# Average pooling 2x2x2: eight loads through one ring, five of them issued by GpSimd

## The chip, the cores and the metric

The kernel runs on one core of a Trainium2 chip. The metric is device time in microseconds, the median of repeated executions. One execution of each kernel is also recorded by the hardware profiler. Its span goes from the first recorded instruction to the last; DMA transfers that are still landing after the last instruction are outside the span but inside the device time.

## The reference

The input `x` has shape (8, 32, 32, 32, 32) in float32, 33.55 MB. Each output element is the mean of a 2x2x2 window; windows don't overlap, so the output is (8, 32, 16, 16, 16), 4.19 MB.

```python
for i in range(out_d):
    for j in range(out_h):
        for k in range(out_w):
            window = x[:, :, 2*i:2*i + 2, 2*j:2*j + 2, 2*k:2*k + 2]
            result[:, :, i, j, k] = np.mean(window, axis=(-3, -2, -1))
```

## The kernel before

Batch and channel together give 256 rows of 128 KB. They are taken as two halves, `t = 0` and `t = 1`, of 128 rows, one row per partition. Along a row the data is cut into units; a unit of `kb` KB is `kb` KB in each of the 128 partitions (`KF` is 1 KB in float32 elements). In the diff and below, (t, k0, kb) is a unit: its half, where it starts in the row, and its length, both in KB.

The list `plan` has eight entries of 32 KB. Each takes one of five buffers of 32 KB from the pool `pin` (`tin` in the profile), 160 KB per partition in all. The last two entries are loaded as two pieces of 16 KB each. So there are ten loads, six of 4 MB and four of 2 MB, all issued by the SP engine on one queue in the order of `plan`. The sixth load and those after it wait until VectorE has finished with the buffer that they overwrite.

For each loaded piece, `pool_unit` runs three steps on VectorE, in place: L58 adds the two planes of a pair (depth), L62 adds neighbours (width), and L65 adds the two rows of a pair (height), scales by 0.125, and writes to the output buffer `obuf0` or `obuf1`. L65 shows in the profile as two entries, the operation itself and a short read of an accumulator that goes to `dummy`. Each of the three steps counts VectorE's semaphore up by one. The scheduler of the framework may move steps of one unit ahead of another's.

Three stores follow on SP, behind all loads: 12 KB of half 1, 16 KB of half 0, and the last 4 KB of half 1. In the output, 1 KB stands for 8 KB of the input, so that 12 KB of half 1 need its first 96 KB of input.

After the program is compiled, its instruction lists are edited by hand: the first load is moved ahead of the opening barrier of the engines, so that SP issues it at once; and the final waits for the three stores are moved behind the closing barrier.

Of the kernel before, what the change touches and what calls it, by code (L numbers as in the profile page):

```python
# [1 line left out]

# [4 lines left out]

F32 = mybir.dt.float32
KF = 256


@with_exitstack
def pool_rows(
    ctx: ExitStack,
    tc: tile.TileContext,
    x: bass.AP,
    kernel_size: int,
    out: bass.AP,
):
    nc = tc.nc  # L20
    assert kernel_size == 2, "only kernel_size == 2 supported"

    B, C, D, H, W = x.shape
    P = nc.NUM_PARTITIONS
    assert (B * C, D, H, W) == (2 * P, 32, 32, 32)
    add = mybir.AluOpType.add

    xv = x.rearrange("b c d h w -> (b c) (d h w)")  # L30
    ov = out.rearrange("b c d h w -> (b c) (d h w)")

    pool_in = ctx.enter_context(tc.tile_pool(name="pin", bufs=5))
    pool_out = ctx.enter_context(tc.tile_pool(name="pout", bufs=1))
    obuf = [pool_out.tile([P, 16 * KF], F32, name=f"obuf{t}") for t in range(2)]
    dummy = pool_out.tile([P, 1], F32, name="dummy")


    plan = [
        (0, 0, (32,)),
        (0, 32, (32,)),
        (0, 64, (32,)),
        (0, 96, (32,)),
        (1, 0, (32,)),
        (1, 32, (32,)),
        (1, 64, (16, 16)),
        (1, 96, (16, 16)),  # L50
    ]

    def pool_unit(buf, t, k0, kb):

        od = kb // 8
        a = buf.rearrange("p (o dd e) -> p o dd e", o=od, dd=2)
        b = buf[:, :od * 1024]
        nc.vector.tensor_add(  # L58
            out=b.rearrange("p (o e) -> p o e", o=od), in0=a[:, :, 0], in1=a[:, :, 1])
        bv = b.rearrange("p (e ww) -> p e ww", ww=2)  # L60
        c = buf[:, od * 1024:od * 1536]
        nc.vector.tensor_add(out=c, in0=bv[:, :, 0], in1=bv[:, :, 1])  # L62
        cv = c.rearrange("p (j hh k) -> p j hh k", hh=2, k=16)
        o0 = k0 * KF // 8
        nc.vector.tensor_tensor_reduce(  # L65
            out=obuf[t][:, o0:o0 + od * 256].rearrange("p (j k) -> p j k", k=16),
            in0=cv[:, :, 0], in1=cv[:, :, 1],
            scale=0.125, scalar=0.0, op0=add, op1=add, accum_out=dummy[:, :],
        )

    for t, k0, parts in plan:
        tin = pool_in.tile([P, 32 * KF], F32, tag="tin", name="tin")
        views = []
        o = 0
        for kb in parts:
            v = tin[:, o * KF:(o + kb) * KF]
            nc.sync.dma_start(
                out=v, in_=xv[t * P:(t + 1) * P, (k0 + o) * KF:(k0 + o + kb) * KF])
            views.append((v, k0 + o, kb))
            o += kb  # L80
        for v, k, kb in views:
            pool_unit(v, t, k, kb)

    for t, k0, kb in [(1, 0, 12), (0, 0, 16), (1, 12, 4)]:
        nc.sync.dma_start(
            out=ov[t * P:(t + 1) * P, k0 * KF:(k0 + kb) * KF],
            in_=obuf[t][:, k0 * KF:(k0 + kb) * KF],
        )  # L90


def kernel(tc: tile.TileContext, x: bass.AP, kernel_size: int, out: bass.AP):
    nc = tc.nc
    pool_rows(tc, x, kernel_size, out)
    tc.close()
    tc.compile()  # L97
    blocks = nc.main_func.blocks

    opening, program = blocks[0].instructions, blocks[tc.starting_block_idx].instructions
    load = next(i for i in program if isinstance(i, mybir.InstDMACopy))
    assert load.engine == nc.sync.engine
    barrier = next(
        n for n, i in enumerate(opening)
        if i.engine == load.engine and isinstance(i, mybir.InstDrain))
    program.remove(load)
    opening.insert(barrier, load)

    closing = blocks[-1].instructions
    stores = [
        i for i in program
        if isinstance(i, mybir.InstDMACopy) and "out_" in i.outs[0].memref]
    kept = [u.id for i in stores for u in i.sync_info.on_update]
    final = next(
        i for i in closing  # L120
        if i.engine == nc.sync.engine and isinstance(i, mybir.InstDrain))
    waits = {w.id: w for w in final.sync_info.on_wait}
    closing[closing.index(final)] = mybir.InstDrain(
        name=final.name, engine=final.engine, ins=[], outs=[], is_reset_sema=False,
        sync_info=mybir.SyncInfo(
            on_wait=[w for n, w in waits.items() if n not in kept], on_update=[]))


    reset = next(
        n for n, i in enumerate(closing)  # L130
        if isinstance(i, mybir.InstDrain) and i.is_reset_sema)
    first, stop = closing[reset].reset_range_start, closing[reset].reset_range_stop
    assert isinstance(closing[reset + 1], mybir.InstISA)
    while len(closing) > reset:
        closing.pop()
    n = first
    while n < stop:
        m = n
        while m < stop and m not in kept:
            m += 1  # L140
        if m > n:
            closing.append(mybir.InstDrain(
                name=nc.get_next_instruction_name(), engine=nc.gpsimd.engine, ins=[], outs=[],
                is_reset_sema=True, reset_range_start=n, reset_range_stop=m))
            nc.gpsimd.sem_clear(range(n, m))
        n = m + 1
    for n in kept:
        w = waits[n]
        closing.append(mybir.InstEventSemaphore(
            name=nc.get_next_instruction_name(), engine=nc.sync.engine, ins=[], outs=[],  # L150
            sync_info=mybir.SyncInfo(
                on_wait=[w],
                on_update=[mybir.SyncUpdate(
                    sync_type="semaphore", id=n, ant_name=w.ant_name,
                    update_mode="sem-sub-imm", update_value=w.wait_value)])))


# [1 line left out]
_INS = ['x', 'kernel_size']  # L159
_OUTS = [((8, 32, 16, 16, 16), 'float32')]  # L160

_NUMBERS = {'kernel_size': 2}


# [26 lines left out]
```

## Time and profile before

| what | value |
|---|---|
| device time, median of 15 runs | 91.41 us (91.29 to 91.92) |
| device time of the profiled execution | 91.3 us |
| its span | 86.4 us |
| VectorE busy | 64.0 us |
| GpSimd busy | 0.2 us (four memsets at the start) |
| first load landed, first VectorE step | 12.08 us |
| median issue to landing, 4 MB loads / 2 MB loads | 34.9 / 38.0 us |
| last VectorE step ends | about 85.2 us |

How to read it: the last instruction in the span is on VectorE; the stores that depend on it are issued by SP and land after the span. The time from issue to landing of a load is mostly time in the queue behind earlier loads, since SP issues several ahead.

### The profile page before, as it was taken

Reading aid. Unit: us, or ns where it says so; the run is one execution under the profiler, and the core shown is the slowest. Engines: PE = TensorE matmul, PEld = TensorE weight load, DVE = VectorE, ACT = ScalarE, POOL = GpSimd, SP = SyncE. Lnnn points to the kernel's source line nnn. Section 1 sums busy time; section 2 is a strip of 40 time slices with the busy share of each in tenths; the row PEclk is TensorE's granted clock in tenths of the full one; section 3 lists DMA queues with packets and bytes.
Section 4 is the critical chain, followed back from the end, with each engine's and each line's share of the span. In section 5 each row is a group of like instructions: output and inputs, shape, how many; then the busy total and the mean of one; then the engine's idle time right before and its main releaser. Section 6 shows DMA issues by size and latency. Waiting matters only on the chain.

```text
span 86.4 us, 89 instructions
## 1 busy us (share of the span) xinstructions
DVE 64.0 (74%) x40; POOL 0.2 (0%) x4
## 2 busy tenths in 40 slices
DVE  0000049993999749992999749992999999999994
POOL 0000000000000000000000000000000000000000
DMA  8979997999979998899979999798999999999999
GB/s 243 410 334 470 486 486 319 410 486 486 455 303 455 486 486 379 364 470 486 486 303 425 486 486 455 303 455 379 470 394 455 410 440 432 417 432 398 444 440 463
DMA packets 1679, 36.68 MB, mean 425 GB/s; under 512 B 176, under 2 KB 176, under 8 KB 176
## 3 DMA queue, kind: packets, MB, share of 16 engines
q1 hardware_dynamic: 1679, 36.68, 99.5%
HBM read 33.55 MB, written 4.19 MB: 437 GB/s over the span
## 4 chain that ended last, share of the span: by engine, by line
DMA 61%; DVE 37%; issue 0%; DVEq 0%
DMA tin<-in_x_dram 61%; DVE tin L58 21%; DVE tin L62 11%; DVE obuf L65 6%; DVE dummy L65 0%; DVEq L97 0%
## 5 line engine op out<-in xcount | busy, mean ns | idle before, releaser
L58 DVE TENSOR_TENSOR tin<-tin 128x4096 f32<-128x4096 f32 (+1 forms) x10 | 35.7, 3569 | 20.6 <-DMA tin<-in_x_dram 20.6
L62 DVE TENSOR_TENSOR tin<-tin 128x2048 f32<-128x2048 f32 (+1 forms) x10 | 18.6, 1864 | 0.3
L65 DVE CUSTOM_DVE_ANT_1 obuf<-tin 128x1024 f32<-128x1024 f32 (+1 forms) x10 | 10.1, 1010 | 0.3
L65 DVE DVE_READ_ACCUMULATOR2_ANT dummy<- 128x1 f32 x10 | 0.8, 82 | 0.0
L172 POOL MEMSET const-uint8-127<- 128x1 uint8 x1 | 0.1, 102 | 0.0
L172 POOL MEMSET const-bfloat16-1.0<- 128x1 bf16 x1 | 0.1, 101 | 0.0
L172 POOL MEMSET const-float32-0.0<- 128x1 f32 x1 | 0.1, 98 | 0.2 <-issue 0.2
L172 POOL MEMSET const-float32-1.0<- 128x1 f32 x1 | 0.1, 98 | 0.0
## 6 DMA issues: line engine op xcount, KB each, us to landing
tin<-in_x_dram SPq DMA_DIRECT2D x6, 4096.0 KB, 34.9
tin<-in_x_dram SPq DMA_DIRECT2D x4, 2048.0 KB, 38.0
out_dram<-obuf SPq DMA_DIRECT2D x1, 2048.0 KB, 11.5
out_dram<-obuf SPq DMA_DIRECT2D x1, 1536.0 KB, 7.0
out_dram<-obuf SPq DMA_DIRECT2D x1, 512.0 KB, 4.7
```

Of the source, the lines that this page charges most:

```text
L58: nc.vector.tensor_add(out=b.rearrange("p (o e) -> p o e", o=od), in0=a[:, :, 0], in1=a[:, :, 1])
L62: nc.vector.tensor_add(out=c, in0=bv[:, :, 0], in1=bv[:, :, 1])
L65: nc.vector.tensor_tensor_reduce(out=obuf[t][:, o0:o0 + od * 256].rearrange("p (j k) -> p j k", k=16), in0=cv[:, :, 0], in1=cv[:, :, 1], s ...
L172: nc = _bacc.Bacc("TRN2", target_bir_lowering=False, num_devices=1)
```

## The change

The five buffers become one buffer `ring` of 160 KB per partition, and each unit names the place in it (`r0`, in KB) where it is loaded. There are eight loads instead of ten. The new plan, in the order in which VectorE takes the units (a new call pins the first step of each unit behind what is already on VectorE):

| unit (t, k0, kb) | place in the ring | issued by |
|---|---|---|
| (0, 32, 48) | 32 to 80 | GpSimd |
| (0, 0, 32) | 0 to 32 | SP |
| (0, 80, 48) | 80 to 128 | GpSimd |
| (1, 0, 32) | 128 to 160 | GpSimd |
| (1, 32, 32) | 0 to 32 | GpSimd |
| (1, 64, 32) | 32 to 64 | GpSimd |
| (1, 96, 16) | 64 to 80 | SP |
| (1, 112, 16) | 80 to 96 | SP |

The GpSimd loads are issued with `single_packet=True`. The load that moves ahead of the opening barrier is the first one of SP, (0, 0, 32).

The stores are the same three pieces in another order: 16 KB of half 0, 12 KB of half 1, 4 KB of half 1.

Two waits are raised by an edit of the instruction list. The second load of SP, (1, 96, 16), waits until VectorE's count is 14 instead of a smaller value. The first store waits for one less than what the second store needs.

```diff
-    pool_in = ctx.enter_context(tc.tile_pool(name="pin", bufs=5))
-    pool_out = ctx.enter_context(tc.tile_pool(name="pout", bufs=1))
+    pool = ctx.enter_context(tc.tile_pool(name="ring", bufs=1))
+    ring = pool.tile([P, 160 * KF], F32, name="ring")
...
     plan = [
-        (0, 0, (32,)),
...
-        (1, 64, (16, 16)),
-        (1, 96, (16, 16)),
+        (0, 32, 48, 32, False),
+        (0, 0, 32, 0, True),
+        (0, 80, 48, 80, False),
+        (1, 0, 32, 128, False),
+        (1, 32, 32, 0, False),
+        (1, 64, 32, 32, False),
+        (1, 96, 16, 64, True),
+        (1, 112, 16, 80, True),
     ]
...
-        nc.vector.tensor_add(
+        first = nc.vector.tensor_add(
             out=b.rearrange("p (o e) -> p o e", o=od), in0=a[:, :, 0], in1=a[:, :, 1])
+        tc.keep_in_program_order(first)
...
+    for t, k0, kb, r0, hw in plan:
+        unit = ring[:, r0 * KF:(r0 + kb) * KF]
+        src = xv[t * P:(t + 1) * P, k0 * KF:(k0 + kb) * KF]
+        if hw:
+            nc.sync.dma_start(out=unit, in_=src)
+        else:
+            nc.gpsimd.dma_start(out=unit, in_=src, single_packet=True)
+        pool_unit(unit, t, k0, kb)
...
-    for t, k0, kb in [(1, 0, 12), (0, 0, 16), (1, 12, 4)]:
+    for t, k0, kb in [(0, 0, 16), (1, 0, 12), (1, 12, 4)]:
...
+    n, load = loads[1]
+    waits = []
+    for w in load.sync_info.on_wait:
+        if w.ant_name.startswith("DVE"):
+            assert w.wait_value < 14
+            w = copy.replace(w, wait_value=14)
+        waits.append(w)
...
+    (n, store), (_, second) = stores[:2]
+    need, = [w for w in second.sync_info.on_wait if w.ant_name.startswith("DVE")]
+    waits = []
+    for w in store.sync_info.on_wait:
+        if w.ant_name.startswith("DVE"):
+            assert w.id == need.id and w.wait_value < need.wait_value - 1
+            w = copy.replace(w, wait_value=need.wait_value - 1)
+        waits.append(w)
```

## The prediction

> **What bounds the kernel now.** I read the shares of busy time first, then the loads' groups, then busy time by stage, then the issues with their landings.
>
> ```profile
> span 86.4 us, 89 instructions
> ...
> DVE 64.0 (74%) x40; POOL 0.2 (0%) x4
> ...
> q1 hardware_dynamic: 1679, 36.68, 99.5%
> HBM read 33.55 MB, written 4.19 MB: 437 GB/s over the span
> ...
> L58 DVE TENSOR_TENSOR tin<-tin 128x4096 f32<-128x4096 f32 (+1 forms) x10 | 35.7, 3569 | 20.6 <-DMA tin<-in_x_dram 20.6
> ```
>
> VectorE works 64.0 of 86.4 us and its idle time is put down to loads. The one DMA queue is full: its packets took 99.5% of 16 engines' span. The stages show whether it ever runs dry (columns: stretch, length, VectorE busy, GpSimd busy, clock, DMA share, GB/s):
>
> ```profile
> 0.00:12.08 12.08, 0.00 (x1) 0.20 (x4) 1.00 0.96 391
> 12.08:21.79 9.71, 7.95 (x4) 0.00 (x0) 1.00 1.00 432
> ...
> 41.22:50.94 9.72, 7.95 (x5) 0.00 (x0) 1.00 1.00 432
> ...
> 60.65:70.00 9.35, 9.31 (x4) 0.00 (x0) 1.00 1.00 426
> 70.00:76.80 6.80, 6.70 (x10) 0.00 (x0) 1.00 1.00 424
> 76.80:80.90 4.10, 4.03 (x5) 0.00 (x0) 1.00 0.99 421
> ```
>
> A stage of 32 KB rows lasts 9.71 us, and VectorE needs 7.95 of it: it waits 1.70 us for each load. From 60.65 on, where rows are 16 KB, the same engines, still full, move 424 instead of 432 GB/s: short rows cost something. Only the first 2.35 us (12.06 to the first landing less 9.71 for 32 KB rows) are start-up. The end, by the timeline (start, length, what):
>
> ```profile
> 76.84 8.73 SPq L87 DMA_DIRECT2D out_dram<-obuf  x3
> ...
> 85.13 0.08 DVE L65 DVE_READ_ACCUMULATOR2_ANT dummy<- 128x1 f32 x1
> ```
>
> and, from the issues (KB of each, median us from issue to landing),
>
> ```profile
> out_dram<-obuf SPq DMA_DIRECT2D x1, 2048.0 KB, 11.5
> ...
> out_dram<-obuf SPq DMA_DIRECT2D x1, 512.0 KB, 4.7
> ```
>
> The 2 MB store is issued at about 77.2 and lands 11.5 us later, at 88.7. The last store is issued at about 85.2 and lands 4.7 us later, at 89.9, behind the other. So the chain of waits, which ends with VectorE at 85.2, isn't the whole end: the queue works until 89.9. The profiled execution took 91.3 us, so 1.4 us lie around this; the median is 91.41, 0.11 more. The kernel is one full stream of DMA.
>
> **What the skill says.** "DMA: Bandwidth & Descriptors", section "Where 436 GB/s comes from", puts the ceiling at 435 GB/s; the 432 here agrees and leaves 0.7%. Its section "Queues, rings and completion order" says that an engine takes turns between the rings that have work, a whole packet from one before it switches. No trace of before shows this: it has one queue. "SBUF — State Buffer", "Who interferes with whom", says that a two-input VectorE add takes only the shared read side and so (it calls this inferred) doesn't hold up GpSimd's descriptor writing; here too nothing of before shows it, and I take it as so.
>
> **The change part by part.** I call the units S0 (32 KB, SP, issued at 0.00 as now), A and B (48 KB), C, D, E (32 KB), all GpSimd, then F and G (16 KB, SP). VectorE takes A, S0, B, C, D, E, F, G.
>
> *Fewer rows.* 32 KB rows run at 432 GB/s, so one row on one of 16 engines takes 32768 x 16 / 432000 = 1.214 us. 16 KB rows at 424: 0.618, 11 ns more than half. So a row costs about 22 ns apart from its bytes if all of that is per row (2 x 0.618 - 1.214); at 426 it is 17 ns. Each engine now has 10 loads x 8 rows = 80, then 8 x 8 = 64. 16 rows x 17 to 22 ns = 0.27 to 0.35 us. The later stages mix in sixteen engines' completions, so I take 0.2, ends 0.1 and 0.35. The stores keep their sizes.
>
> *Single packets.* 40 rows per engine go as five packets. If the gap between rows inside a packet goes away, at most 40 x 17 ns = 0.7 us; the ceiling of 435 allows 0.7% of the 25 MB that GpSimd loads (58 us), 0.4 us. Against it stands whatever each of five loads costs to be taken up from another ring: nothing if the next is queued while the last runs, which holds for B, C (free slots at the start), E and D (slots free at 38.7 and 30.7, below, long before 50). I take a gain of 0.25 us, ends +1.5 (five gaps of 0.3) and -0.4.
>
> *The start.* S0 alone feeds the engines at first: no packet in the first microsecond, sixteen in the second. GpSimd is past its four memsets at 0.43 us; the same page's section "Latency and other measured facts" gives about 1 us to the first byte for such a DMA. So A arrives after one or two rows of S0. As a single packet it then holds each engine for 8 x 1.5 x 1.21 = 14.5 us: 2.35 + 2 x 1.21 + 14.5 = 19.3, I say A lands at 18 to 19.5. S0 and A together are landed by 12.06 + 14.5 = 26.6 if S0's rest comes before B. Then B 41.1, C 50.8, D 60.5, E 70.2, F 75.1, G 80.0 (9.7 for 32 KB, 4.9 for 16). The whole thing stands or falls with "S0's rest before B", which no row of before shows.
>
> *VectorE.* A 32 KB unit occupies 8.0 us (12.08 to 20.11). 48 KB: 4.42 + 2.13, 2.29 + 1.07, 1.22 + 0.53 (each plus the step from half size to full) = 11.7. A 16 KB unit 4.2. A 19.0 to 30.7, S0 to 38.7, B 41.1 to 52.8, C to 60.8, D to 68.8, E 70.2 to 78.2, F to 82.4, G to 86.6. That ends 1.4 us later than now, but the last store needs the queue free: loads end 80.0, the 16 KB store at 84.9, the 12 KB one at 88.6. A store issued at 86.7 has 1.9 us to get its first byte there; the first load of before needed 1.0 to 2. Hidden, barely. If that cover were gone, each microsecond of VectorE would be one of the end.
>
> *Added waits.* F waits for value 14 of VectorE, with three steps per unit the second of D: 60.8 + 6.7 = 67.5. E's data runs until 70.2: 2.7 us to spare, of which issue to data takes 1 to 2. Queued behind F on SP are G and all three stores; none could go earlier with use, G's slot being free at 52.8. The first store waits for 17, the second step of E, 77.0, when F and G still fill the queue until 80.0. So both waits cost nothing in this picture. SP's ordering past F is harmless; GpSimd's D waits for S0 to be consumed, with E behind it.
>
> *The closing.* GpSimd's loads are in the closing waits, all done long before 89.9. Nothing; at most 0.3 us for GpSimd's part in it.
>
> Sum against its own execution: 91.3 - 0.2 - 0.25 = 90.85; against the median, 91.41 - 0.45 = 90.96. I take 90.95.
>
> **Rivals.**
>
> *Nothing measurable.* The rows' cost is smaller and the packets bring nothing: 91.41 - 0.1 = 91.3. For it: 432 of 435. Against: the 424 stages are real.
>
> *Handing over between rings costs.* Five loads that each leave the engines idle 0.2 to 0.3 us, or GpSimd's descriptors arriving late: 91.41 - 0.2 + 1.0 to 1.5 = 92.2 to 92.7. In before, one queue with loads lined up has no such gap; for it speaks that two queues have never been seen here.
>
> *The first unit comes late* (slower). If S0's eight rows count as one packet, or rows of S0 and A alternate, A lands at 26.6, and VectorE, which takes A first, starts there. Then A 38.3, S0 46.3, B 58.0, C 66.0, D's second step 72.7: only now is F issued, with the engines idle since 70.2. F's data starts about 74.2, G ends 84.0, stores 88.9, 92.6 and 93.9, and 1.4 around: 95.3. It decides from the point where D's second step ends past 70.2 - 1.5 = 68.7, that is where A lands after 68.7 - 46.1 = 22.6; each microsecond later costs one. Against: A's packet is meant to go through whole.
>
> *S0 starves.* The turn-taking, read strictly, gives S0 one row after A, one after B: S0 lands after C, at 50.8, VectorE idles from 31, D's load waits for S0's end at 58.8, runs 60.3 to 70, E to 79.7; D's second step is at 85.2, F and G run 86.7 to 96.5, stores to 106.4, in all 107.8.
>
> **How the numbers follow.** Forecast (90.5 to 91.2): 0.50. Nothing measurable: 0.12. Handing over (91.6 to 93): 0.16. First unit late (93 to 95.5): 0.14. S0 starves (above 100): 0.08. A measurement of this kernel tells about 0.2% from no change, 91.23 to 91.59. Faster is the forecast case, 0.50; same 0.12; slower 0.16 + 0.14 + 0.08 = 0.38. Range: from 90.3, which takes in -0.35 and -0.4 with the median (90.7) and a little of the start, to 94.0, which takes in the handing over and the nearer part of the late first unit; left out are starving, 0.08, and most of the late unit, about 0.1. Of the likeliest case alone: 90.5 to 91.2.
>
> **What would show it.** Right: A's first step starts at 18 to 20 us, S0's right behind it with no idle time, every stretch from 12 to 85 at 432 GB/s or above, F issued while E still lands, the last store landing at 89.4 to 89.7. Wrong: a first step at 24 or later; an idle stretch of VectorE between A and S0; a slice with the DMA share under 9 tenths near 70 us, where F is held; GB/s under 430 while GpSimd's loads run; or the last store landing right after its issue, which would mean that VectorE sets the end.

## The result and the profile after

The changed kernel takes 97.02 us (median of 9 runs, 96.80 to 97.17) where the kernel before takes 91.37 (median of 47). The ratio is 1.061, 95% interval 1.0595 to 1.0623: 5.65 us slower, where 0.45 us faster was forecast. The profiled execution took 97.16 us, its span is 91.4.

The page of the changed kernel, the lines that answer to those of before:

```profile
span 91.4 us, 78 instructions
...
DVE 63.1 (69%) x32; POOL 3.0 (3%) x9
...
q0 software_dynamic: 720, 25.17, 63.9%
q1 hardware_dynamic: 631, 11.16, 30.9%
HBM read 33.55 MB, written 4.19 MB: 413 GB/s over the span
...
L60 DVE TENSOR_TENSOR ring<-ring 128x4096 f32<-128x4096 f32 (+2 forms) x8 | 35.4, 4421 | 26.7 <-DMA ring<-in_x_dram 26.6
```

There are two queues now, and together they fill 94.8% of the engines' span in place of 99.5%. VectorE's idle time is 26.7 us, more than before (20.6), but of another shape: nearly all of it is one single wait at the start. The timeline (start, length, what; in brackets the idle time before it and what ended it) shows it, and what follows from it:

```profile
0.00 73.43 SPq L78 DMA_DIRECT2D ring<-in_x_dram  x3
...
1.29 1.71 POOL L80 DMA_DIRECT2D ring<-in_x_dram  x3 [0.85 <-PEq L95]
26.65 6.56 DVE L60 TENSOR_TENSOR ring<-ring 128x6144 f32<-128x6144 f32 x1 [26.65 <-DMA ring<-in_x_dram]
...
70.30 2.29 DVE L65 TENSOR_TENSOR ring<-ring 128x2048 f32<-128x2048 f32 x1
...
80.56 10.12 SPq L85 DMA_DIRECT2D out_dram<-obuf  x3
...
86.03 2.29 DVE L60 TENSOR_TENSOR ring<-ring 128x2048 f32<-128x2048 f32 x1
```

The first step starts at 26.65. From there to 90.3 VectorE works with next to no break, so that everything it releases comes late. The second step of unit D ends at 72.6, and only then does SP issue F (at 72.62; G follows at 73.07). The stages show what the engines do meanwhile (stretch, length, VectorE busy, GpSimd busy, clock, DMA share, GB/s):

```profile
4.00:20.00 16.00, 0.00 (x0) 0.00 (x0) 1.00 1.02 440
```

```profile
69.50:73.10 3.60, 3.53 (x3) 0.00 (x0) 1.00 0.00 0
73.10:75.00 1.90, 1.90 (x3) 0.00 (x0) 1.00 0.81 190
75.00:82.00 7.00, 6.93 (x5) 0.00 (x0) 1.00 1.02 435
82.00:86.00 4.00, 3.93 (x4) 0.00 (x0) 1.00 0.99 315
86.00:91.40 5.40, 4.21 (x4) 0.00 (x0) 1.00 0.98 421
```

At the start the engines are as full as before. Then two losses stand out. From 69.5 to 73.1 no row starts, and the restart in the next stretch is slow (190 GB/s). (A stage counts a row where it starts. By the single rows of the trace, E's last ones end at 70.0 and F's first ones start at 73.6 to 74.2 and take 1.0 to 1.7 us, where 0.61 is usual.) From 82 to 86 the engines are busy at only 315 GB/s. In bytes, against 432: 3.6 us whole, 1.9 x (1 - 190/432) = 1.1 us and 4.0 x (1 - 315/432) = 1.1 us, in all 5.8, close to the 5.65 that were lost.

Why the first step is so late shows in the DMA view of the stretch from 4 to 20 us (queue, packets, MB, share of 16 engines), and in S0's time from its issue at 0.00 to its landing:

```profile
q0 software_dynamic: 80, 3.93, 56.7%
q1 hardware_dynamic: 95, 3.11, 45.0%
...
ring<-in_x_dram SPq DMA_DIRECT2D x1, 4096.0 KB, 22.8
```

GpSimd's queue (q0) and SP's (q1) get about the same number of rows, 80 and 95. The rows of the trace show the turns themselves. On one engine, for example, rows of A start at 5.20, 8.22, 11.24, 14.26 and 17.28, and rows of S0 between them, at 7.01, 10.03, 13.05, 16.07 and 19.09, each where the row of the other queue ends. A's first row starts at 5.2 to 6.9 us, after three or four rows of S0. S0 lands at 22.8 and A at 26.6: the two together are just when the forecast had them, but neither is early.

### The profile page after: what moved, and what is told of

Read it like the earlier page. It is cut to its first block, busy times and chain, and to the rows that moved or that the text cites. A ratio compares the mean times of both kernels' runs of the same rounds, so it can differ in the third digit from the quotient of the medians.

```text
span 91.4 us, 78 instructions
## 1 busy us (share of the span) xinstructions
DVE 63.1 (69%) x32; POOL 3.0 (3%) x9
## 4 chain that ended last, share of the span: by engine, by line
DVE 55%; DMA 42%; issue 1%; SPq 0%; PEldq 0%; DVEq 0%
DMA ring<-in_x_dram 42%; DVE ring L60 31%; DVE ring L65 16%; DVE obuf L68 7%; SPq L78 0%; DVE dummy L68 0%; PEldq L95 0%; DVEq L95 0%
## 5 line engine op out<-in xcount | busy, mean ns | idle before, releaser
L60 DVE TENSOR_TENSOR ring<-ring 128x4096 f32<-128x4096 f32 (+2 forms) x8 | 35.4, 4421 | 26.7 <-DMA ring<-in_x_dram 26.6
L65 DVE TENSOR_TENSOR ring<-ring 128x2048 f32<-128x2048 f32 (+2 forms) x8 | 18.3, 2292 | 0.3
L68 DVE CUSTOM_DVE_ANT_1 obuf<-ring 128x1024 f32<-128x1024 f32 (+2 forms) x8 | 9.8, 1226 | 0.3
L80 POOL DMA_DIRECT2D ring<-in_x_dram x5 | 2.8, 555 | 44.5 <-DVE dummy L68 43.6
## 6 DMA issues: line engine op xcount, KB each, us to landing
ring<-in_x_dram SPq DMA_DIRECT2D x1, 4096.0 KB, 22.8
out_dram<-obuf SPq DMA_DIRECT2D x1, 2048.0 KB, 10.3
```

The costliest lines, as they stand in the source:

```text
L60: first = nc.vector.tensor_add(out=b.rearrange("p (o e) -> p o e", o=od), in0=a[:, :, 0], in1=a[:, :, 1])
L68: nc.vector.tensor_tensor_reduce(out=obuf[t][:, o0:o0 + od * 256].rearrange("p (j k) -> p j k", k=16), in0=cv[:, :, 0], in1=cv[:, :, 1], s ...
L80: nc.gpsimd.dma_start(out=unit, in_=src, single_packet=True)
```

## The experiments

The first experiments vary the changed kernel in one thing at a time, the later ones in more; the units keep their names S0, A to G. Each ratio is to the kernel before on the same chip.

**The flag.** Taken off the five GpSimd loads:

```diff
-            nc.gpsimd.dma_start(out=unit, in_=src, single_packet=True)
+            nc.gpsimd.dma_start(out=unit, in_=src)
```

> The changed kernel with the flag for one packet taken off the five GpSimd loads. Theory (the two rings alternate row by row, whatever the flag says, so the first unit of VectorE lands at 26.6 us): nothing moves, first VectorE step at 26.6 us, 96.7 to 97.3 us. Rival (the flag shapes the order or the gaps between rows): the first step moves by over 1 us or the time by over 0.5 us.

Measured: 96.99 us, ratio 1.0612 (1.0597 to 1.0627), first step at 26.54. The flag decides neither the order nor the time here. Nor does it change the pace of the rows, which the time alone wouldn't show: from A's landing to E's, with GpSimd's loads alone on the engines, it takes 43.68 us with the flag and 43.65 without (by the traces' marks of when a load has landed).

**VectorE's order.** VectorE takes S0 before A; no other line moves.

```diff
-        (0, 32, 48, 32, False),
         (0, 0, 32, 0, True),
+        (0, 32, 48, 32, False),
```

> The changed kernel, but VectorE takes the SP unit of 32 KB first and the 48 KB unit second. Theory: first step at 22.8 us where that unit lands, VectorE 3.8 us earlier all through, the hold ends near 69 us, the empty stretch shrinks to about 1.2 us; 92.4 to 93.7 us. Rival (the order of VectorE doesn't matter, GpSimd's loads do): 96 us or more.

Measured: 93.61 us, ratio 1.0237 (1.0207 to 1.0268), as expected, with the first step at 23.18. Exchanging two lines of the plan takes back 3.4 us of 5.65. The loads that wait for VectorE go out sooner with it: D at 31.49 and E at 43.16 in place of 46.62 and 47.14, F at 69.16 in place of 72.62, before E has landed (70.46). Slow rows are left at F's start and from 78 to 81.

**The hold of F.** First without it:

```diff
-            w = copy.replace(w, wait_value=14)
```

> The changed kernel without the raised wait (14) of SP's second load. Theory (late first unit, and the hold then leaves the engines without data from 69.5 to 73.6 us): the empty stretch goes, VectorE still starts at 26.6 and ends at about 90.3, last store about 2.5 us after that, 93.5 to 94.5 us. Rival (the loss lies in the GpSimd loads themselves or in the handing over): 96 us or more.

Measured: 100.57 us, ratio 1.1007 (1.0990 to 1.1024). Here the expectation was plainly wrong. The stages of this kernel:

```profile
68.50:80.00 11.50, 7.95 (x4) 0.00 (x0) 1.00 0.87 373
80.00:82.00 2.00, 1.95 (x1) 0.00 (x0) 1.00 0.00 0
82.00:86.80 4.80, 4.76 (x2) 0.00 (x0) 1.00 0.00 0
```

and two lines of its timeline:

```profile
68.50 4.43 DVE L60 TENSOR_TENSOR ring<-ring 128x4096 f32<-128x4096 f32 x1 [2.65 <-DMA ring<-in_x_dram]
...
80.05 4.42 DVE L60 TENSOR_TENSOR ring<-ring 128x4096 f32<-128x4096 f32 x1 [3.53 <-DMA ring<-in_x_dram]
```

F and G, now free to go early (issued at 38.35 and 56.15), take every second row while C, D and E are loaded. D and E land 2.65 and 3.53 us after VectorE wants them, and with all loads in at 80, the held first store leaves the engines empty until 86.8. So the row-wise turns hurt at both ends of the kernel; the expectation had followed them at the start and left them out here. To see whether the held store makes it worse, the kernel with neither raised wait:

> The changed kernel with neither raised wait. Theory (each ring gets every second row, so whatever SP issues early comes out of GpSimd's loads): the 16 KB store, free to go from about 58 us, now also alternates with GpSimd's last load, which lands near 83 us in place of 80; VectorE ends about 3 us later than with the store held, 102.5 to 104 us. Rival (an engine kept busy is never worse): faster than the 100.6 us of the kernel with the store held, since the engines no longer run dry from 80 to 87 us.

Measured: 104.17 us, ratio 1.1414 (1.1397 to 1.1431), just above the top of what was expected. E's first step waits longer still:

```profile
83.99 4.42 DVE L60 TENSOR_TENSOR ring<-ring 128x4096 f32<-128x4096 f32 x1 [7.44 <-DMA ring<-in_x_dram]
```

Here DMA engines kept busy with the wrong rows cost more than empty ones. With the hold at 12 in place of 14, F comes when E is already under way:

> The changed kernel with the raised wait of SP's second load at 12 instead of 14, which VectorE reaches about 7 us sooner, at 65.9 us. Theory: the load's rows are there when GpSimd's last load ends near 70 us, so the empty stretch of 4 us goes; but VectorE, which starts at 26.6 and never waits, still ends at 90.3 and now sets the end: last store about 2.6 us later, 93.9 to 94.5 us. Rival (the rest of the loss is in GpSimd's loads, not in VectorE's late start): 96 us or more; rival (the wait is all of it): 91.5 us or less.

Measured: 94.21 us, ratio 1.0312 (1.0295 to 1.0330), as expected. The empty stretch at 70 is gone:

```profile
69.50:73.50 4.00, 3.93 (x3) 0.00 (x0) 1.00 1.02 434
```

What remains is VectorE's late start: its last unit ends at 90 and the last store lands 2.7 us after its issue, about as soon as in the two experiments before this one (2.6). So 14 was a value for a VectorE that is about 7 us earlier than it is.

**Both repairs.** S0 first and the hold at 13:

> The changed kernel with both repairs: VectorE takes the SP unit of 32 KB first, and the raised wait is 13, near 66.9 us. Theory: no empty stretch and VectorE early enough, so the stream of DMA sets the end again: 91.2 us, or up to 92.3 if the rows near 80 to 82 us are slow as they were in the kernels with two rings. Rival (loads through GpSimd cost time of their own): 92.5 us or more.

Measured: 91.41 us, ratio 1.0004 (0.9990 to 1.0018). All of the 5.65 us is gone, with the five loads still on GpSimd. The second queue as such costs nothing that can be told from no change, and it brings nothing either. The late first unit and the wait that is too late for it are the cause of the loss: each repair alone takes back a part (to 93.61 and 94.21), both together all. (The slow rows from 82 to 86 go with them; what makes such rows is a question of its own, further down.)

**One queue.** All eight loads on SP (`True` in the plan stands for SP), the hold of F left out; then the same with S0 first.

```diff
-        (0, 32, 48, 32, False),
+        (0, 32, 48, 32, True),
         (0, 0, 32, 0, True),
-        (0, 80, 48, 80, False),
...
+        (0, 80, 48, 80, True),
...
```

> The changed kernel with all eight loads on SP, in the same order, and without the hold of 14, which belongs to the second queue: ring, unit sizes, order of VectorE and held first store stay. Theory: one queue takes the rows in order, the 48 KB unit lands at about 17 us, the engines never run dry, 16 rows fewer: 90.9 to 91.3 us. Rival (unit sizes, ring or held store cost something themselves): 92 us or more.

> All eight loads on SP, and the 32 KB unit first, so that VectorE starts at 12 us. Theory: the one stream sets the end and VectorE's start doesn't matter as long as it is before about 22 us: within 0.2 us of the same kernel with the 48 KB unit first, 91.0 to 91.4 us.

Measured: 91.23 us, ratio 0.9984 (0.9965 to 1.0003), and 91.20 us, ratio 0.9988 (0.9973 to 1.0004). In one queue A lands at 16.9, ahead of S0:

```profile
16.91 6.56 DVE L60 TENSOR_TENSOR ring<-ring 128x6144 f32<-128x6144 f32 x1 [16.91 <-DMA ring<-in_x_dram]
```

VectorE can start at 16.9 or, with S0 first, at 12.0 with the same time. The gain over before, 0.15 us, is the size of the forecast's first term, but neither interval excludes none.

**The price of a row.** The kernel before with sixteen loads of 16 KB rows:

```diff
-        (0, 0, (32,)),
+        (0, 0, (16, 16)),
```

and so for all entries.

> The kernel before with all sixteen loads in 16 KB rows: 48 rows more on each engine. Theory (a row costs 11 ns apart from its bytes, from the stages of before): 0.5 us more, 91.8 to 92.0; at the 17 to 22 ns of the prediction 0.8 to 1.05 us more, 92.2 to 92.5. Rival (rows cost nothing measurable): 91.3 to 91.5 us.

Measured: 92.61 us, ratio 1.0141 (1.0124 to 1.0158), 1.3 us more and above all that was expected. Most of that isn't the rows. Its timeline:

```profile
12.21 2.29 DVE L58 TENSOR_TENSOR tin<-tin 128x2048 f32<-128x2048 f32 x1 [0.58 <-DMA tin<-in_x_dram]
...
61.15 2.29 DVE L58 TENSOR_TENSOR tin<-tin 128x2048 f32<-128x2048 f32 x1 [0.61 <-DMA tin<-in_x_dram]
...
66.80 2.29 DVE L58 TENSOR_TENSOR tin<-tin 128x2048 f32<-128x2048 f32 x1 [1.36 <-DMA tin<-in_x_dram]
```

From 12.21 to 61.15 ten loads come at 4.894 us each, 9.788 for 32 KB in place of before's 9.71: 0.074 us for 8 rows, 9 ns a row, 0.44 us for 48. One load, at 66.80, comes 0.75 us late. The page of this kernel has a line for a queue of its own:

```profile
q14 instruction: 1, 0.01, 0.0%
```

By the rows of the trace, one of the 16 engines moved this packet, 8 KB of instructions, at 64.72, and its next row took 1.27 us in place of 0.61. Fifteen engines were through with the load by 66.02, this one at 66.78, and VectorE had to wait for the last. It stays as far behind until the last load (81.44, the others by 80.70). The rows and this packet make 1.2 of the 1.3 us. One execution was traced, so that the packet comes there every time isn't shown; the four times, 92.47 to 92.71, agree with it. Nine ns times the 16 rows that the change saves are 0.15 us.

**The slow rows from 82 to 86.** The first guess was that the first store's issue, at 80.56, disturbs the last load, so that without its raised wait the slow stretch would move with it:

> The changed kernel without the raised wait of the first store, which then goes out right behind SP's last load, at about 73.5 us. Theory: the store stands in the same ring behind the loads, so that the order of rows is the same and the time within 0.3 us of the changed kernel's. Open: rows of the last load took about 1 us in place of 0.6 near 82 to 85 us, soon after the stores were issued; if the issue of the first store causes it, that stretch moves to about 75 us; if the second store or something else does, it stays.

Measured: 97.03 us, ratio 1.0619 (1.0601 to 1.0637), the time that was expected. The store went out at 73.43, and the slow rows stayed (295 GB/s from 82 to 84, 344 to 86). The second guess was the restart after an empty stretch. In one queue, with a wait for 16 put on F to make such a stretch:

> All eight loads on SP (one ring), with a wait for VectorE's count of 16 added to the first 16 KB load, reached at about 74.9 us, while the load before it lands near 70 us. Theory: an empty stretch from 70 to about 75.6 us costs its length and the restart, with no GpSimd in it: 96.8 to 98.0 us. Open: if rows about 9 us after the restart are slow here too, the slow rows of the changed kernel belong to a restart and not to the second ring. Rival (stores and VectorE have slack for it): under 94 us.

Measured: 99.28 us, ratio 1.0879 (1.0856 to 1.0901), 1.3 us above what was expected, which had no slow rows in it. Empty engines cost their length also without GpSimd, and the slow rows are there (270 GB/s from 84 to 86), so the second queue isn't needed for them. That fitted a restart. But the one-queue kernel with S0 first and without the store's raised wait has no restart:

> Ring, eight loads and new order of stores, all loads on SP with the 32 KB unit first, and no raised wait at all. Theory: in one ring the held store changes nothing, and 16 rows fewer on each engine at 9 ns give 0.15 us: 91.1 to 91.3 us, 0.1 to 0.2 us under the kernel before. Rival: the held store was needed to keep the loads ahead, 91.5 us or more.

Measured: 91.95 us, ratio 1.0060 (1.0039 to 1.0081), 0.75 us more than with the store held (91.20; 0.65 by the two ratios), and slow rows again. Both guesses were wrong. What the kernels with slow rows shared was a first store issued 5 us or more before its data could start: in the changed kernel 10.3 us from issue to landing, less 4.9 for 2 MB, is 5.4. Two runs move the issue one step each way, later in the changed kernel and earlier in the one-queue kernel:

```diff
-            w = copy.replace(w, wait_value=need.wait_value - 1)
+            w = copy.replace(w, wait_value=need.wait_value)
```

> The changed kernel with the first store held one step longer, to 18, about 1.2 us later (81.75 us). Theory (rows of the last load become slow when a store has been waiting behind them for over about 4 us; it is 5.4 us in the changed kernel): the wait of the store falls to about 3.3 us, the slow rows go, the last load lands 1 us earlier: 95.8 to 96.3 us. Rival (the slow rows have another cause): 96.8 to 97.2 us as before.

```diff
-            w = copy.replace(w, wait_value=need.wait_value - 1)
+            w = copy.replace(w, wait_value=need.wait_value - 2)
```

> All loads on SP, 32 KB unit first, with the first store held to 16 instead of 17, so that it is issued about 2.3 us sooner, near 74.7 us, and waits about 5.4 us behind the last load's rows. Theory: slow rows appear, 91.7 to 92.0 us. Rival (the store's early issue matters only when it is very early, or chance made the difference of 0.75 us between held and not held): 91.1 to 91.4 us.

Measured: 95.87 us, ratio 1.0485 (1.0441 to 1.0529), and 92.06 us, ratio 1.0059 (1.0038 to 1.0080). Both went as the theory said, the second 0.06 us past its range. In the changed kernel with the store at 81.87, the rows of the last load run at full speed:

```profile
82.00:84.00 2.00, 2.00 (x1) 0.00 (x0) 1.00 0.96 410
84.00:86.00 2.00, 1.93 (x5) 0.00 (x0) 1.00 1.09 467
```

And the same stretch of the one-queue kernel with S0 first, the store held to 17,

```profile
77.00:80.00 3.00, 2.97 (x4) 0.00 (x0) 1.00 0.98 421
```

and held to 16:

```profile
77.00:80.00 3.00, 2.99 (x3) 0.00 (x0) 1.00 0.98 306
```

Three us at 306 in place of 421 are 0.8 us, about the difference of the two times (92.06 and 91.20; 0.65 by the ratios). So the early issue of the first store brings the slow rows, in one queue and in two.

The other kernels fit. Take the first store's time from issue to landing, less what its bytes need (4.9 us for 2 MB, 3.7 for 1.5 MB). In seven of the sixteen kernels this wait is 1.4 to 3.3 us, and there are no slow rows ahead of the store. In eight it is 5.0 us or more, up to 1.0 us of it made by the slow rows themselves, and they are there. The kernel before with 16 KB rows lies between. Its page gives 9.1 - 3.7 = 5.4, but only for the engine that is behind; for the other fifteen it is 4.7. A few of its rows took up to 0.88 us, and its stages from 76 to 84 stay above 400 GB/s.

The slow rows need not be in the store's own queue. In the kernel with neither raised wait the store, issued at 58.0, has its first rows at 75.4, and in the 3.4 us before that the rows of GpSimd's last load are slow, two on each engine, 1.4 to 1.8 us each in place of 1.21:

```profile
72.00:75.40 3.40, 3.33 (x3) 0.00 (x0) 1.00 0.94 304
```

## Why the prediction was wrong

**What bounds it.** Right: the stream of DMA sets the time in the kernel before. The kernels whose engines are neither empty nor slow take 91.2 to 91.4 (three variants do). The forecast of the stream was good as well: B, C, D and E land at 41.2, 50.9, 60.6 and 70.3, where it had 41.1, 50.8, 60.5 and 70.2. The closing costs 1.4 us after the last landing, as before.

**The step that failed** is in *The start*: "As a single packet it then holds each engine for 8 x 1.5 x 1.21 = 14.5 us", so that "A lands at 18 to 19.5". A landed at 26.6, because the rows of the two queues alternate. In the run without the flag VectorE starts at 26.54, so the flag was no reason for A to pass. The section "Queues, rings and completion order" of the Trainium skill's page "DMA: Bandwidth & Descriptors" has the engine take turns by packets. That there are turns, the trace confirms; that eight rows of one load go as one packet, it does not: 80 rows of one queue to 95 of the other, one by one. Whether the flag makes no packet of such rows or the engine switches inside one, no run here tells.

The same paragraph took about 1 us to the first byte, so that A would come after one or two rows of S0. It came after three or four: its issue starts at 1.29, its first rows at 5.2 to 6.9. This alone would have done little. With the prediction's 14.5 us from there, A would by estimate have been through at 19.7 to 21.4, still before the 22.6 that the prediction gives as the point where the hold of F begins to cost.

Between a whole A ahead of S0's rest, turns row by row and a starved S0, no row of before could decide. The forecast took the first and gave the case with the turns 0.14. That case was worked out on record, and the runs bear out its mechanism: first step at 26.6, F issued at 72.7 (measured 72.62), the engines idle from 70. It gave 95.3, where 97.02 came. Of the missing 1.7 us, 1.15 are the slow rows (97.02 less the 95.87 with the store one step later); the rest, about 0.6, is about what F's first rows lost, which took 1.30 us on the mean in place of 0.61.

**Added waits.** "So both waits cost nothing in this picture" fell with the picture. F's wait would by the prediction's sum have had 2.7 us to spare with A at 19 (whether 2.7 are enough isn't shown: with GpSimd's rows running, F's first rows came 3.0 to 4.8 us after its issue); with A at 26.6 it cost the whole empty stretch. But it is no plain cost: without it the kernel takes 100.57. The first store's wait was put at nothing as well. As it stands it is nothing in the changed kernel (97.03 without it), but one step more would have brought 1.15 us, and in one queue it is worth about 0.7.

**Fewer rows.** 0.2 us was taken; at the measured 9 ns a row it is 0.15, and the one-queue kernels show 0.15, which isn't clear of noise. The prediction's 17 to 22 ns a row was read off single stages, whose GB/s jump by whole rows. A stretch of 20 us of the kernel before, with 32 KB rows alone, can read 419 as well:

```profile
30.00:50.00 20.00, 15.90 (x8) 0.00 (x0) 1.00 0.97 419
```

**Single packets.** 0.25 us was taken; none shows. From A's landing to E's it takes 43.68 us with the flag, 43.65 without, and 43.74 in the one-queue kernel with S0 first; and the repaired kernel on two queues, 91.41, is no faster than the one-queue kernel, 91.20. Of its costs the forecast was right: the five loads on the other queue cost 0.2 us in these two, which can't be told from none.

**VectorE.** Its steps were sized right (48 KB: 6.56, 3.36 and 1.76 us). From the Trainium skill's "SBUF — State Buffer", "Who interferes with whom", the prediction took that VectorE's adds don't hold up GpSimd's issues, which the page calls inferred. This case agrees: the later two issues, in the middle of an add at 46.62, take 1.05 us for both, 0.53 each, where the first three took 0.53 to 0.66.

## What to carry to other kernels

Before moving loads to a second queue, ask which rows will share the engines with which: what is issued early on one queue comes out of what is needed next on the other, and of two loads that share the engines row by row neither is early (S0 at 22.8 and A at 26.6, where one queue has its first load in at 12.0 or 16.9). Where two queues must be used, let the consumer take what lands first, and set every hand-made wait from the landing times of that very kernel: the same wait was worth 3.5 us against early rows (100.57 to 97.02) and cost 2.8 us by being two steps too late (97.02 to 94.21). In a kernel whose DMA engines never rest, look for empty and slow stretches in the windows first: in the changed kernel all that was lost stands in two such stretches.

## What the runs showed of the hardware

- Rows of two queues alternated one for one on the engines, whatever their size (32 KB against 48 KB: 95 and 80 in 16 us), with the single-packet flag or without.
- The first rows of SP's load F came 1.0 to 1.8 us after its issue on idle engines (hold at 14), and 3.0 to 4.8 us after it while GpSimd's rows were running (hold at 12, at 13 with S0 first, and no hold).
- In the 3 us before a store's first rows, the rows on the engines slowed down (16 KB rows from 0.61 to about 0.9 us on the mean) when the store had been waiting in its queue for about 5 us or more. With a wait of 3.3 us or less they didn't. It cost 0.65 to 1.15 us. Issuing the store later, by one step of VectorE, made it go in the changed kernel; issuing it earlier, by one step, made it come in the one-queue kernel. Why is not known, nor where between 3.3 and 5.0 us it begins.
- In the kernel with 16 KB rows one of the 16 engines moved an 8 KB packet of instructions and was 0.75 us behind from then on. Each load landed with its last engine, so that every later load landed that much later (66.78 where the other fifteen had 66.02).
